# An encoder layer's branch B: output stores one unit later, splits and loads held ahead of the next unit's softmax, projection A one unit later

## The chip, the cores and the metric

The kernel runs on one core of a Trainium2 chip. The metric is the device time of one execution in microseconds (us).

## The reference

One layer of an encoder with two token mixers, applied on its own to a prompt of 1024 tokens and to a sample of 512, both 1024 wide, in float32. Cut to what matters:

```python
z = rmsnorm(x) @ W_in          # q_A k_A v_A | q_B k_B v_B (8 heads of 64) | gate_A gate_B
o_A = grouped_query_attention(rope(norm(q_A)), rope(norm(k_A)), v_A)
# branch B: per head, 128 queries against a band of rows of a 64-column grid
s = q_B . k_B[band] * 64**-0.5 + rel_pos_bias[head, dr, dc]
s = where(window(8 rows x 16 columns), s, -1e30)
o_B = softmax(s) @ v_B[band]
x = x + (sigmoid(gate_A) * (o_A @ W_pA) + sigmoid(gate_B) * (o_B @ W_pB)) @ W_out
x = x + relu(rmsnorm(x) @ W_up)**2 @ W_down
y = rmsnorm(x)
```

## The kernel before

Every float32 operand of a matmul is kept as two parts: `hi`, the value rounded by ACT (ScalarE), and `lo`, the rest, computed by DVE (VectorE). `split` (L183) makes the two, and `mm3` (L201) does a product as three matmuls. Activations lie transposed, 128 features by up to 512 tokens.

The short trunk (512 tokens, `NB == 1`) runs first, then the long one (1024 tokens, `NB == 2`), then the feed-forward part of both. A trunk does branch A in two passes, then branch B in a phase of its own (the pool `phB` at L871), then the output projection. The change acts in branch B, above all in the long trunk's, which the trace shows from about 773 to 1083 us.

Branch B is a loop over 32 units, a head `h` and a quarter `j` of the columns, with three kinds of steps, each for another unit:

- `s_unit` (L972): the scores `sbs` on PE (TensorE), bias added and the row's maximum taken on DVE (`sbss`, L1002), the exponential on ACT (`pbs`, L1024 or L1034), the division by the row's sum on POOL (GpSimd, L1037). The bias plus mask, `bms`, is added on POOL (L983).
- The turn of the probabilities, which the next product needs transposed. Heads 6 and 7 do it on PE (`ptbs`, L1076). In the long trunk heads 0 to 5 (the set `moved`, 24 units) take a detour: a 32 by 32 transpose on DVE (`turn`, L1046), a copy to DRAM issued by POOL (`tbs`, L1048), and in the next turn of the loop a fetch by four DMAs of SP (SyncE) that puts the blocks in their places (`fetch_t`, L1056, three buffers `bhs`). `t_unit` splits what was fetched, `hi` on ACT (L1066) and `lo` on DVE (L1067), three units after the scores.
- `v_unit` (L1087): the product with the values, `obs` on PE, four units after the scores; `finish_o` (L441) then adds two halves of it on ACT and DVE (`ot_Bs`, `os_Bs`) and stores the output (`obds`, L461) through `store[0]`, which is SP in the detour.

Between these steps PE is given filler work by `Fill.pull` (L48), three matmuls a pull: first branch B's gate, `gate(3328)` (matmuls `gpss`, weights `w_gs` in eight tiles, result `sgs` written by ACT and stored as `zgs` by SP), then projection A, `proj_a` (L832, matmuls `ppas`, weights `w_pas`, inputs `oXs`). A unit of head h whose index is 6 or 7 modulo 8 also does half of the query and key projections of the next two heads (`qkproj` L913, `pqbs`, `pkbs`, splits `qBs` and `kBs`). The weights and the inputs `oXs` come as raw float32 by SP into a ring of three raw tiles and are split from there; for `oXs` this is `load_o` (L818), and `oa_held` is the list of splits still to be made. `prep_v` (L894) loads a unit's values `vss`, four DMAs on SP.

Each engine does its instructions in the order that it is given. A scheduler decides this order, except where `tc.keep_in_program_order` pins it. In the long trunk's loop all matmuls are pinned (`held_pe`), so PE follows the program's text, and a late input stops it. ACT, DVE, POOL and SP are ordered by the scheduler, apart from the pins that the text shows.

Of the kernel before, what the change touches and what calls it, by code (L numbers as in the profile page):

```python
# [61 lines left out]
def encoder(ctx: ExitStack, tc: tile.TileContext, xs, outs, w):  # L62
# [119 lines left out]

    def split(hi, lo, src, pin=False):  # L183
        op = nc.scalar.activation(hi, src, AF.Copy)  # L184
        if pin:
            tc.keep_in_program_order(op)
        n = src.shape[1]
        cut = [0, n // 2, n] if n % 2 == 0 else [0, n]
        for a, b in zip(cut, cut[1:]):
            op = nc.vector.tensor_tensor(lo[:, a:b], src[:, a:b], hi[:, a:b].bitcast(F32), op=ALU.subtract)  # L190
            if pin:
                tc.keep_in_program_order(op)

    held_pe = []
# [21 lines left out]
    def load_cols(src, off, ncol, name, alloc=None, pin=False, hold=None, raw_of=None):  # L216
# [9 lines left out]
        for k0 in range(0, nk, kp):  # L226
# [3 lines left out]
            op = nc.sync.dma_start(rv, v[:, k0 : k0 + kn, off : off + ncol])  # L230
            if pin:
# [171 lines left out]
    def run(tr, nxt, first):  # L403
# [10 lines left out]
        store = [nc.scalar]  # L414

# [25 lines left out]
        def finish_o(o, n, dst, pool, nm, parts=None):  # L441
# [8 lines left out]
            else:  # L450
                nc.scalar.activation(t[:, :n], o[HD:P, :n], AF.Copy)
            if parts is not None:
                hi, lo, ps = parts
                b = pool.tile([P, n], F32, tag="os", name=f"os_{nm}", bufs=2)[ps, :n]
# [4 lines left out]
            b = pool.tile([HD, n], F32, tag="os", name=f"os_{nm}", bufs=2)  # L459
            nc.vector.tensor_tensor(b[:, :n], o[0:HD, :n], t[:, :n], op=ALU.add)  # L460
            store[0].dma_start(dst, b[:, :n])  # L461
# [356 lines left out]
        def load_o(br, hold=None, raw_of=raw_tile):  # L818
            parts = []
            for k in range(4 - br):  # L820
                raw = raw_of(f"rawo{N}_{br}_{k}")
                nc.sync.dma_start(raw[:, :T], (oad, obd)[br][k * P : (k + 1) * P, :])
                t = slot([P, 2, T], F32R, f"oX{N}_{br}_{k}", first and br + k == 0)
                cut = partial(split, t[:, 0, :], t[:, 1, :], raw[:, :T], br == 0 and NB == 2)
                if hold is None:
                    cut()
                else:
                    hold.append(cut)
# [42 lines left out]
        with phase(f"phB{N}") as ph:  # L871
# [41 lines left out]
            def qkproj(pr, wqk, dest):  # L913
# [4 lines left out]
                for tb in range(NB):  # L918
# [5 lines left out]
                    for e in range(2):  # L924
# [11 lines left out]
                        late = NB == 2 and (pr, tb) == (3, 1)  # L936
                        op = nc.scalar.activation(dst_h, src, AF.Copy, scale=0.125)
                        if late:
                            tc.keep_in_program_order(op)
                        for jj in range(4):  # L940
                            op = nc.vector.scalar_tensor_tensor(
# [7 lines left out]
                            if late:  # L949
                                tc.keep_in_program_order(op)  # L950
# [4 lines left out]
                    for e in range(2):  # L955
# [4 lines left out]
                        for os_ in both:  # L960
                            op = nc.scalar.activation(kT[e][os_, 0, cs], pk[hs], AF.Copy)
                            if NB == 2 and (pr, tb) == (3, 1):
                                tc.keep_in_program_order(op)
# [8 lines left out]
            def s_unit(u, before=None):  # L972
# [25 lines left out]
                for hf in range(halves):  # L998
# [3 lines left out]
                    nc.vector.tensor_tensor_reduce(  # L1002
                        out=sb,
                        in0=s[:, hf * 512 : hf * 512 + nkey],
                        in1=bms[hf],
                        op0=ALU.add,
                        op1=ALU.min,
                        scale=-1.0,
                        scalar=3e38,
                        accum_out=nm_,  # L1010
                    )
# [7 lines left out]
                for hf, (sb, nm_) in enumerate(sums):  # L1019
                    nm = f"{N}_{h}_{j}_{hf}"  # L1020
                    l = sml.tile([P, 1], F32, tag="l", name=f"lb{nm}")
                    if u in moved:
                        p = pm[:, :, hf]
                        nc.scalar.activation(  # L1024
                            p.rearrange("p b k i -> p k b i"),
                            sb.rearrange("p (k b i) -> p k b i", b=4, i=32),
                            AF.Exp,
                            bias=nm_,
                            scale=-1.0,
                            accum_out=l,  # L1030
                        )
                    else:
                        p = pm[:, hf * nkey : (hf + 1) * nkey]
# [888 lines left out]
```

## Time and profile before

| | us |
|---|---|
| median of three runs | 2165.71 |
| lowest, highest | 2163.8, 2169.11 |
| the profiled execution | 2162.64 |
| its span, first to last instruction | 2160.9 |
| TensorE's mean granted clock in it | 0.994 |

The time of an execution is its span and 1.7 us around it. The profile's busy times and waits are from that one execution. A row of an engine's timeline gives the start and the duration in us, the engine and line, the operation with output and inputs by the program's names, the shape, the number of instructions and, in brackets, how long the engine was idle before and what released it. A row of the waits view groups such idle times by the instruction that waited and the one that it waited for. Instructions that only issue a DMA belong to a queue, SPq for SyncE.

### The profile page before, as it was taken

Reading aid. Unit: us, or ns where it says so; the run is one execution under the profiler, and the core shown is the slowest. Engines: PE = TensorE matmul, PEld = TensorE weight load, DVE = VectorE, ACT = ScalarE, POOL = GpSimd, SP = SyncE. Lnnn points to the kernel's source line nnn. Section 1 sums busy time; section 2 is a strip of 40 time slices with the busy share of each in tenths; the row PEclk is TensorE's granted clock in tenths of the full one; section 3 lists DMA queues with packets and bytes.
Section 4 is the critical chain, followed back from the end, with each engine's and each line's share of the span. In section 5 each row is a group of like instructions: output and inputs, shape, how many; then the busy total and the mean of one; then the engine's idle time right before and its main releaser. Section 6 shows DMA issues by size and latency. Waiting matters only on the chain.

```text
span 2160.9 us, 32004 instructions
## 1 busy us (share of the span) xinstructions
PE 2104.1 (97%) x10871; PEld 1841.4 (85%) x10871; DVE 1484.3 (69%) x2793; ACT 1140.5 (53%) x2487; POOL 377.0 (17%) x470
## 2 busy tenths in 40 slices
PE   9999999999999999987999999999999999999998
PEld 8888778988898878865888899998999988888886
DVE  6665786777657746765882777777777777659662
ACT  6664654666556645544540566566555643434342
POOL 2332310332223224542200200003000000000000
PEclk9999999999999999998999999999999999999999
DMA  6437557521221146675563655578444799688561
GB/s 192 129 106 217 156 157 244 174 71 33 59 85 53 39 111 189 195 205 153 174 209 126 221 179 180 185 230 229 144 158 156 245 351 340 216 274 283 170 204 59
DMA packets 337003, 372.95 MB, mean 173 GB/s; under 512 B 33472, under 2 KB 269640, under 8 KB 336840
## 3 DMA queue, kind: packets, MB, share of 16 engines
q1 hardware_dynamic: 296695, 296.17, 44.2%
q10 hardware_dynamic: 31072, 45.11, 5.9%
q0 software_dynamic: 9072, 29.63, 4.7%
q8 instruction: 86, 1.41, 0.3%
q14 instruction: 78, 0.63, 0.1%
HBM read 274.29 MB, written 97.32 MB: 172 GB/s over the span
## 4 chain that ended last, share of the span: by engine, by line
PE 66%; DVE 1%; DMA 1%; issue 1%; ACT 1%; POOL 0%; SPq 0%; POOLq 0%; ACTq 0%; DVEq 0%
PE dn L197 20%; PE ua L197 6%; PE ud L197 6%; PE uc L197 6%; PE gpss L197 5%; PE ops L197 4%; PE ub L197 3%; PE ppbs L197 2%; PE pkbs L197 2%; PE pqbs L197 2%; PE ppas L197 2%; PE dnf L197 2%; PE pTs L791 1%; PE obs L197 1%; PE sbs L197 1%
## 5 line engine op out<-in xcount | busy, mean ns | idle before, releaser
L197 PE MATMUL dn<-wd,ah 128*128 128x512 f32 x1248 | 384.3, 389 | 0.0
L197 PEld LDWEIGHTS dn<-wd,ah 128*128 128x128 f32 x1248 | 234.4, 188 | 48.5
L197 PE MATMUL dn<-wd,al 128*128 128x512 f32 x624 | 243.0, 389 | 0.0
L1396 ACT ACTIVATE ah<-ar 128x512 fp32r<-128x512 f32 x168 | 104.1, 627 | 197.7 <-PE dn L197 183.3
L197 PE MATMUL gpss<-xs_0h,w_gs 128*128 128x512 f32 x512 | 189.3, 405 | 5.1 <-ACT w_gs L184 3.8
L1397 DVE TENSOR_TENSOR al<-ar,ah 128x512 fp32r<-128x512 f32 x168 | 114.5, 690 | 74.0 <-ACT ah L1396 63.6
L197 PE MATMUL ud<-B,A 128*128 128x384 f32 x768 | 143.7, 335 | 0.7 <-DVE c L1514 0.7
L197 PE MATMUL uc<-B,A 128*128 128x384 f32 x768 | 143.7, 334 | 0.0
L197 PE MATMUL ua<-B,A 128*128 128x384 f32 x768 | 138.8, 334 | 0.0
L197 PEld LDWEIGHTS dn<-wd,al 128*128 128x128 f32 x624 | 117.2, 188 | 24.3
L757 POOL TENSOR_SCALAR ps<-ps,rls 128x1024 f32<-128x1024 f32 (+1 forms) x96 | 96.9, 1010 | 225.5 <-DVE rls L756 200.2
L197 PEld LDWEIGHTS ud<-B,A 128*128 128x128 f32 x768 | 134.0, 188 | 1.1 <-DVE c L1514 1.1
L197 PEld LDWEIGHTS uc<-B,A 128*128 128x128 f32 x768 | 134.1, 188 | 0.2 <-ACT A L1396 0.2
L197 PEld LDWEIGHTS ua<-B,A 128*128 128x128 f32 x768 | 133.7, 188 | 0.2
L797 DVE TENSOR_TENSOR ptls<-pTs,pths 128x512 fp32r<-128x512 f32 x160 | 107.7, 687 | 37.6 <-ACT pths L796 36.8
L796 ACT ACTIVATE pths<-pTs 128x512 fp32r<-128x512 f32 x160 | 94.0, 597 | 74.0 <-PE pTs L791 71.7
L197 PE MATMUL ops<-wh_os,mgs 128*128 128x512 f32 x384 | 119.5, 391 | 0.0
L197 PEld LDWEIGHTS gpss<-xs_0h,w_gs 128*128 128x128 f32 x512 | 96.8, 190 | 24.6 <-ACT w_gs L184 4.5
L751 DVE TENSOR_REDUCE nms<-ss 128x1 f32<-128x1024 f32 (+1 forms) x96 | 99.9, 1041 | 25.5 <-PE ss L749 25.0
L180 POOL TENSOR_TENSOR rs_f<-ms_f,mhalf 128x1 f32<-128x1 f32 x6 | 4.0, 667 | 590.7 <-DVE ms_f L176 590.7
L754 ACT ACTIVATE ps<-ss,nms 128x1024 f32<-128x1024 f32 (+1 forms) x96 | 93.2, 972 | 22.7 <-DVE nms L751 20.1
L791 PEld LDWEIGHTS pTs<-ident,ps 128*128 128x128 f32 x640 | 77.9, 140 | 28.3 <-POOL ps L757 4.1
(290 smaller groups left out, 5164.6 us busy)
## 6 DMA issues: line engine op xcount, KB each, us to landing
ar<-ud SPq DMA_DIRECT2D x120, 512.0 KB, 5.1
br<-in_w_mlp_down_dram SPq DMA_DIRECT2D x72, 512.0 KB, 5.5
rawu<-in_w_mlp_up_dram SPq DMA_DIRECT2D x64, 512.0 KB, 4.1
ud<-c ACTq DMA_DIRECT2D x128, 192.0 KB, 2.9
raw_gs<-in_w_in_dram SPq DMA_DIRECT2D x32, 512.0 KB, 4.1
ud<-cs SPq DMA_DIRECT2D x64, 192.0 KB
tbs<-pbs POOLq DMA_DIRECT2D x24, 384.0 KB, 3.5
bhs<-tbs SPq DMA_DIRECT2D x96, 96.0 KB, 2.5
```

What stands on the lines that cost most here:

```text
L180: nc.gpsimd.tensor_tensor(r[:, :n], m[:, :n], mhalf[:, :n], op=ALU.pow)
L197: op = nc.tensor.matmul(out, a, b, **kw)
L751: nc.vector.tensor_reduce(nm_, s, axis=AX.X, op=ALU.max, negate=True)
L754: nc.scalar.activation(p, s, AF.Exp, bias=nm_, accum_out=l)
L757: nc.gpsimd.tensor_scalar(p, p, rl, 1.0, op0=ALU.mult, op1=ALU.mult)
L791: nc.tensor.transpose(pt[:, j * P : (j + 1) * P], PP[u, j][:, kc * P : (kc + 1) * P], ident)
L796: nc.scalar.activation(hi, pt, AF.Copy)
L797: nc.vector.tensor_tensor(lo, pt, hi.bitcast(F32), op=ALU.subtract)
L1396: nc.scalar.activation(hi, src, AF.Copy)
L1397: nc.vector.tensor_tensor(lo, src, hi.bitcast(F32), op=ALU.subtract)
```

## The change

It changes the order in which branch B's work is written, and which parts of that order the scheduler must keep. No matmul is added or removed.

1. **Output stores a unit later.** In the detour `finish_o` puts its store on a list, `later_put`; the loop issues it at its end, after `fetch_t`, and keeps the last one back until the next unit.
2. **Splits and raw loads held.** `note` records the instructions of `split` on ACT and DVE and the raw loads on SP. `behind(engine)` puts the next unit's softmax (its sum on DVE, its exponential on ACT), its fetch and its value loads on SP behind all that was recorded on that engine since.
3. **`load_o`.** In the long trunk the raw loads of pieces 2 and 3 of `oXs` are issued when pieces 0 and 1 have been split. The pins on the last query and key splits and on the `oXs` splits are gone, and so are the three `oXs` splits that stood ahead of the end of the last `qkproj`.
4. **Filler.** Nine gate matmuls (`fill.pull(3)`) stand ahead of the first unit. A unit then gets 5 pulls, one in six gets 4 (before: 5, one in three 6). Projection A is set up at unit 22 (before 23) and enters the filler at unit 25 (before 24); in the tail a unit gets 8 pulls (before 7). The `oXs` splits are made from unit 23 on, two per unit in the long trunk (before: one from unit 21). In the short trunk the same line makes them from unit 23, one per unit.

The core of the diff:

```diff
+    @contextmanager
+    def behind(engine):
+        with ExitStack() as st:
+            for ins in firm[engine]:
+                st.enter_context(tc.issue_after(ins))
+            yield
+        firm[engine].clear()
...
-            store[0].dma_start(dst, b[:, :n])
+            if store[0] is nc.scalar:
+                nc.scalar.dma_start(dst, b[:, :n])
+            else:
+                later_put.append((dst, b[:, :n]))
...
-                cut = partial(split, t[:, 0, :], t[:, 1, :], raw[:, :T], br == 0 and NB == 2)
+                def ask(k=k, t=t):
+                    raw = raw_of(f"rawo{N}_{br}_{k}")
+                    note("SP", nc.sync.dma_start(raw[:, :T], (oad, obd)[br][k * P : (k + 1) * P, :]))
+                    return partial(split, t[:, 0, :], t[:, 1, :], raw[:, :T])
...
+                elif NB == 1 or k < 2:
+                    hold.append(ask())
                 else:
-                    hold.append(cut)
+                    cuts = []
+                    early = hold[k - 2]
+                    def then(early=early, ask=ask, cuts=cuts):
+                        early()
+                        cuts.append(ask())
+                    hold[k - 2] = then
+                    hold.append(lambda cuts=cuts: cuts.pop()())
...
-                    nc.vector.tensor_tensor_reduce(
+                    with behind("DVE"):
+                        nc.vector.tensor_tensor_reduce(
...
+                    with behind("ACT"):
+                        nc.scalar.activation(to, of, AF.Exp, bias=nm_, scale=-1.0, accum_out=l)
...
+                with behind("SP"):
+                    for b in range(4):
+                        nc.sync.dma_start(
...
                 held_pe.append(1)
+                fill.pull(3)
...
-                    f = (5 if i < 2 else 2 + i % 2) if NB == 1 else 5 + (i % 3 == 0)
+                    f = (5 if i < 2 else 2 + i % 2) if NB == 1 else 5 - (i % 6 == 5)
                 else:
-                    f = 3 + i % 2 if NB == 1 else 7
-                if NB == 2 and i == n - 9:
+                    f = 3 + i % 2 if NB == 1 else 8
+                if NB == 2 and i == n - 10:
                     pa = proj_a(ph, raw_here)
                     next(pa)
-                    f = 2
...
-                        if NB == 2 and i == n - 9:
-                            for _ in range(NC8):
-                                next(qp)
-                            for _ in range(3):
-                                oa_held.pop(0)()
...
-                if NB == 2 and i == n - 8:
+                if NB == 2 and i == n - 7:
...
-                if oa_held and i > n - 12:
+                if oa_held and i >= n - 9:
                     oa_held.pop(0)()
...
                     fetch_t(units[i - 1])
+                if NB == 2 and oa_held and i >= n - 9:
+                    oa_held.pop(0)()
+                while len(later_put) > (i < n):
+                    nc.sync.dma_start(*later_put.pop(0))
```

What this does to the order shows at three places. The first is ACT in the long trunk's branch B around the last keys, before; `kBs_3_0` and `kBs_3_1` are the split keys of heads 6 and 7, `oXs_0_k` the inputs of projection A.

```order
L447 ACTIVATE ot_Bs_4_3_11495<-obs_4_3_11488 64x512
L1066 ACTIVATE bhs_5_2_11341<-bhs_5_2_11341 128x768
L184 ACTIVATE w_pas_0_11348<-raw_pas_0_0_11346 128x512
L184 ACTIVATE oXs_0_0_11351<-rawos_0_0_11349 128x1024
L184 ACTIVATE oXs_0_1_11354<-rawos_0_1_11352 128x1024
L937 ACTIVATE qBs_3_11244<-pqbs_3_1_11401 64x4x128
L184 ACTIVATE oXs_0_2_11357<-rawos_0_2_11355 128x1024
L937 ACTIVATE qBs_3_11244<-pqbs_3_1_11401 64x4x128
L961 ACTIVATE kBs_3_0_11245<-pkbs_3_1_11445 64x512 x2
L961 ACTIVATE kBs_3_1_11246<-pkbs_3_1_11445 64x512
```

The same place in the changed kernel:

```order
L1091 ACTIVATE bhs_5_1_11176<-bhs_5_1_11176 128x768
L199 ACTIVATE oXs_0_0_11185<-rawos_0_0_11186 128x1024
L971 ACTIVATE qBs_3_11226<-pqbs_3_1_11368 64x4x128 x2
L991 ACTIVATE kBs_3_0_11227<-pkbs_3_1_11403 64x512 x2
L199 ACTIVATE w_pas_0_11184<-raw_pas_0_0_11182 128x512
L991 ACTIVATE kBs_3_1_11228<-pkbs_3_1_11403 64x512
L464 ACTIVATE ot_Bs_4_3_11461<-obs_4_3_11454 64x512
L1091 ACTIVATE bhs_5_2_11322<-bhs_5_2_11322 128x768
```

Three `oXs` splits and one of `w_pas` stood ahead of the keys of `pkbs_3_1`; now one `oXs` split does, the `w_pas` split stands between the two heads' keys, and the output of unit `4_3` follows. On PE, between the last matmul of `pkbs_3_1` and `sbs_6_1`, six gate matmuls and the six of `obs_4_3` stood before; now twelve gate matmuls and those six stand there.

The second place is ACT a little further on, where projection A begins on PE: the output of unit `5_1`, the last gate result `sgs_3328_7_1`, and what follows them, before.

```order
L447 ACTIVATE ot_Bs_5_1_11549<-obs_5_1_11542 64x512
L437 ACTIVATE sgs_3328_7_1_11564<-gpss_3328_7_1_11318 128x512
L1066 ACTIVATE bhs_5_0_11501<-bhs_5_0_11501 128x768
L184 ACTIVATE w_pas_1_11569<-raw_pas_1_0_11567 128x512
L184 ACTIVATE oXs_0_3_11360<-rawos_0_3_11358 128x1024
```

And in the changed kernel, where PE does `ppas_0_0` right behind the last three matmuls of `gpss_3328_7_1`:

```order
L464 ACTIVATE ot_Bs_5_1_11553<-obs_5_1_11546 64x512
L454 ACTIVATE sgs_3328_7_1_11608<-gpss_3328_7_1_11519 128x512
L1091 ACTIVATE bhs_5_0_11466<-bhs_5_0_11466 128x768
L199 ACTIVATE oXs_0_1_11188<-rawos_0_1_11189 128x1024
L199 ACTIVATE oXs_0_2_11191<-rawos_0_2_11446 128x1024
L464 ACTIVATE ot_Bs_5_2_11600<-obs_5_2_11593 64x512
L199 ACTIVATE oXs_0_3_11192<-rawos_0_3_11474 128x1024
```

The splits of `oXs_0_1` and `oXs_0_2` have moved behind the last gate result, and `oXs_0_3` stands behind the output of unit `5_2`.

The third place is SP at the fetches of head 4, before; `obds` is the store of an output, `bhs` the fetch of turned probabilities.

```order
L461 DMA obds_4664<-os_Bs_3_0_10986 64x256
L1056 DMA bhs_4_2_10989<-tbs_4_2_10929 32x4x192 x4
L900 DMA vss_4_10802<-vds_4660 32x4x128 x4
L438 DMA zgs_1_4662<-sgs_3328_6_0_11033 128x512
L461 DMA obds_4664<-os_Bs_3_3_11058 64x256
L1056 DMA bhs_4_0_11061<-tbs_4_0_11010 32x4x192 x4
```

The same in the changed kernel:

```order
L1080 DMA bhs_4_1_10885<-tbs_4_1_10838 32x4x192 x4
L1228 DMA obds_4664<-os_Bs_3_1_10818 64x256
L935 DMA vss_4_10783<-vds_4660 32x4x128 x4
L1080 DMA bhs_4_2_10956<-tbs_4_2_10907 32x4x192 x4
L1228 DMA obds_4664<-os_Bs_3_2_10883 64x256
```

Before, the store of `os_Bs_3_0` stands ahead of the fetch of `bhs_4_2`; now that fetch stands ahead of the store of an older unit, `os_Bs_3_2`, and a store follows a fetch every time.

More of the change, by code (lines that the diff above doesn't have):

```diff
@@ L181, in rstd, with note @@
         return r
+    held_pe = []
+    firm = {"ACT": [], "DVE": [], "SP": []}
+    def note(engine, op):
+        if held_pe:
+            firm[engine].append(op.ins)
+    @contextmanager
[5 more added lines that the diff above has]
+        firm[engine].clear()
     def split(hi, lo, src, pin=False):
         op = nc.scalar.activation(hi, src, AF.Copy)
+        note("ACT", op)
         if pin:
@@ L1054, in fetch_t @@
                 turned = PT[u].rearrange("(a i) b w -> b i a w", i=32)
-                for b in range(4):
-                    nc.sync.dma_start(
-                        hl[b * 32 : b * 32 + 32, 1].rearrange("p a f k i -> p a (f k i)").bitcast(F32), turned[b]
-                    )
+                with behind("SP"):
+                    for b in range(4):
+                        nc.sync.dma_start(
+                            hl[b * 32 : b * 32 + 32, 1].rearrange("p a f k i -> p a (f k i)").bitcast(F32),
+                            turned[b],
+                        )
                 PT[u] = hl
@@ L1158, in run @@
                     if moved and h > 0:
-                        prep_v(h, j)
+                        with behind("SP"):
+                            prep_v(h, j)
                     if i % 8 == 6 and i + 2 < n:
```

62 lines of the change are left out of this document (24 added, 38 removed).

## The prediction

> **What bounds the kernel now.** I read the page's engine table first, then the waits of the tensor engine in the stretch that holds the long trunk's branch B, then that stretch cut into windows, and last the instructions of the engines around the largest waits.
>
> The page's span and its row for the tensor engine (busy time, share, instructions):
>
> ```profile
> span 2160.9 us, 32004 instructions
> PE 2104.1 (97%) x10871; PEld 1841.4 (85%) x10871; DVE 1484.3 (69%) x2793; ACT 1140.5 (53%) x2487; POOL 377.0 (17%) x470
> ```
>
> PE is the bound: only 2160.9 − 2104.1 = 56.8 us of the span are idle. A change that neither adds nor removes matmuls can win only from those, and from time at a lowered clock. How much lies where the change acts is one row of the windows view (length, then busy time of PE, PEld, DVE, ACT, POOL, the granted clock, DMA share and GB/s), and the two largest groups of PE's waits there (total, times, longest):
>
> ```profile
> 770.00:1090.00 320.00, 290.56 (x1361) 241.75 (x1360) 208.68 (x500) 150.18 (x299) 116.82 (x145) 0.97 0.60 176
> PE sbs L197 <- ACT kBs L961: 11.5, 2, 10.2
> PE obs L197 <- issue: 5.9, 3, 2.5
> ```
>
> 320.00 − 290.56 = 29.4 us idle, over half of all idle time. DVE, ACT and POOL are far from full, so each wait is a matter of order. PE's own rows place the waits above 0.5 us, and one below (start, duration, idle before and its releaser in brackets):
>
> ```profile
> 796.77 0.44 PE L197 MATMUL sbs<-kBs,qBs 128*128 128x384 f32 x1 [1.28 <-ACT kBs L961]
> 798.18 0.80 PE L197 MATMUL sbs<-kBs,qBs 128*128 128x384 f32 x3 [0.97 <-DVE kBs L965]
> 798.82 0.39 PE L197 MATMUL gpss<-xs_0h,w_gs 128*128 128x512 f32 x1
> 799.04 0.39 PE L197 MATMUL gpss<-xs_0l,w_gs 128*128 128x512 f32 x1
> ...
> 933.47 0.50 PE L197 MATMUL gpss<-xs_0h,w_gs 128*128 128x512 f32 x1 [0.92 <-ACT w_gs L184]
> 939.99 0.97 PE L197 MATMUL obs<-bhs,vss 128*128 128x256 f32 x6 [1.74 <-issue]
> 946.86 0.95 PE L197 MATMUL obs<-bhs,vss 128*128 128x256 f32 x6 [1.75 <-issue]
> 954.42 0.95 PE L197 MATMUL obs<-bhs,vss 128*128 128x256 f32 x6 [2.46 <-issue]
> 958.99 0.50 PE L197 MATMUL gpss<-xs_0h,w_gs 128*128 128x512 f32 x1 [2.90 <-ACT w_gs L184]
> 960.05 0.84 PE L197 MATMUL gpss<-xs_0h,w_gs 128*128 128x512 f32 x2 [0.33 <-DVE w_gs L190]
> 1005.99 0.69 PE L197 MATMUL sbs<-kBs,qBs 128*128 128x384 f32 x1 [10.20 <-ACT kBs L961]
> 1007.41 1.33 PE L197 MATMUL sbs<-kBs,qBs 128*128 128x384 f32 x3 [0.73 <-DVE kBs L965]
> 1018.78 1.52 PE L197 MATMUL ppas<-oXs,w_pas 128*128 128x512 f32 x2 [3.82 <-ACT oXs L184]
> 1039.26 0.96 PE L197 MATMUL obs<-bhs,vss 128*128 128x512 f32 x4 [1.50 <-DVE bhs L1084]
> ```
>
> Two gate matmuls in a row start 799.04 − 798.82 = 0.22 us apart (0.227 over a longer run); that is the price of a filler matmul as cover.
>
> **The first unit.** At 796.77 PE has just finished the keys of head pair 0 and must wait 1.28 + 0.97 = 2.25 us for their splits. The change pulls nine gate matmuls ahead of it: 9 × 0.227 = 2.05 us of work that was to be done anyway. **−2.05 us**; without that cover, 0.
>
> **The gate's weights.** 0.92 + 2.90 + 0.33 = 4.15 us are waits for splits of w_gs, which the scheduler had put behind a softmax. After, a split stands ahead of the next unit's softmax on ACT and DVE, and with fewer gate matmuls per unit the seventh weight tile is split well before its first use (the order has it twelve gate matmuls and a projection later). **−4.15 us**; I see no other end above 0.9, the smallest of the three.
>
> **The largest wait.** ACT's rows ahead of 1005.99, and the sync engine's queue that held them:
>
> ```profile
> 995.83 0.59 ACT L447 ACTIVATE ot_Bs<-obs 64x512 f32<-64x512 f32 x1 [8.19 <-PE obs L197]
> 996.33 0.83 ACT L1066 ACTIVATE bhs<-bhs 128x768 fp32r<-128x768 f32 x1
> 997.58 1.99 ACT L184 ACTIVATE oXs<-rawos 128x1024 fp32r<-128x1024 f32 x2
> 1003.05 1.06 ACT L184 ACTIVATE oXs<-rawos 128x1024 fp32r<-128x1024 f32 x1 [2.87 <-DMA rawos<-oads]
> 1004.75 1.19 ACT L961 ACTIVATE kBs<-pkbs 64x512 fp32r<-64x512 f32 x2
> 999.19 0.32 SPq L822 DMA_DIRECT2D rawos<-oads  x1
> ```
>
> The copies of the last keys (1004.75) stand behind three oXs splits, and the third waits 2.87 us for a load that SP could only issue at 999.19, when a raw buffer came free. PE, in order, waits 10.20 + 0.73 = 10.93 us. After, one oXs split is ahead of the keys and the loads for the others are asked later; between the last key matmul and sbs stand twelve gate matmuls and six obs matmuls, about 12 × 0.227 + 0.95 = 3.7 us. What they must cover is a w_pas split, the key copies and their lower halves; at the first unit the same stretch was 2.25 us after almost no cover. So **−10.9 us**; at worst the 2.25 of the first unit comes back, −8.7.
>
> **The obs waits of heads 3 and 4.** 1.74 + 1.75 + 2.46 = 5.95 us. Their probabilities travel softmax, transpose, store, fetch, split, obs. Two rows say what delays that chain: SP's queue behind the output store, and the softmax behind the copy-out of its own buffer.
>
> ```profile
> SPq L461 <- DVE os_Bs L460: 28.8, 8, 9.9
> ACT pbs L1024 <- DMA tbs<-pbs: 19.7, 8, 6.9
> 924.28 0.45 SPq L461 DMA_DIRECT2D obds<-os_Bs  x1
> 924.91 1.90 SPq L1056 DMA_DIRECT2D bhs<-tbs  x4
> ```
>
> The store at 924.28 waits for an output, and the four fetches at 924.91 queue behind it although they need it not. After, the fetch goes first and the store is one unit old. That is worth some 2 to 3 us of lead per unit, and the fetched tiles are split a unit ahead of their use. Against it: sbs's softmax is now held behind the w_gs_6 and w_bqs_3 splits, and on POOL two bias sums stand ahead of the store of head 4's first unit. The second row's wait does not go away with that. Following the new order with the durations above, I find obs_3_3 some 3.0 us late and obs_4_1 some 1.9 late: 4.9. **−1.05 us**, between −4 (only 2 us stay) and +1.5 (three units as late as the one at 954.42, 7.4 us).
>
> **The first projection.** Now 3.82 us at 1018.78. In the new order ppas_0_0 follows the last three gate matmuls directly, and ACT's queue between that last gate and the projection's inputs is: sgs, a bhs split, oXs_0_1, oXs_0_2, ot_5_2, oXs_0_3. From the last gate's start: 0.39 to its end (798.82), for sgs about the 0.59 of an output copy, 0.83 for bhs (996.33), 1.04 each for the first two oXs (1003.05), 0.59 (995.83), 1.06, and DVE's lower halves:
>
> ```profile
> L190 DVE TENSOR_TENSOR oXs<-rawos,oXs 128x512 fp32r<-128x512 f32 x8 | 5.2, 682 | 1.9 <-ACT oXs L184 1.9
> ```
>
> 5.2 / 8 = 0.65 each, behind a softmax sum and an output merge. The first half of oXs_0_3 is there some 8 us after the last gate, ppas_0_0 ends at 8.6, and undisturbed it would end at 2.97: 5.6 us instead of 3.82. **+1.8 us**, from 0 to +5 if the raw loads land late too; and +0.5 for the second w_pas (0 to 1.5).
>
> **The tail.** The 1.50 at 1039.26 is a wait for the split of a turned tile; with eight pulls instead of seven per unit more ppas matmuls stand between. **−0.7 us**, half of it either way.
>
> **The clock.** Windows of 10 us around the waits:
>
> ```profile
> 940.00:950.00 10.00, 8.25 (x43) 7.02 (x44) 6.15 (x15) 4.17 (x9) 6.57 (x8) 1.00 0.77 226
> 960.00:970.00 10.00, 9.95 (x40) 8.32 (x41) 4.49 (x12) 2.64 (x7) 2.55 (x2) 0.83 0.39 111
> 990.00:1000.00 10.00, 5.79 (x29) 4.73 (x27) 3.51 (x7) 4.15 (x6) 0.00 (x0) 0.90 0.38 134
> 1000.00:1010.00 10.00, 3.28 (x11) 2.88 (x12) 7.88 (x21) 4.12 (x7) 0.63 (x1) 0.50 0.83 236
> 1010.00:1020.00 10.00, 6.18 (x21) 4.47 (x20) 5.26 (x10) 5.03 (x10) 1.96 (x3) 0.84 0.68 197
> 1020.00:1030.00 10.00, 10.00 (x47) 8.36 (x47) 5.30 (x13) 1.83 (x5) 3.35 (x4) 0.90 0.43 126
> ```
>
> Busy time by (1 − clock): 9.95 × 0.17 + 5.79 × 0.10 + 3.28 × 0.50 + 6.18 × 0.16 + 10.00 × 0.10 = 5.9 us of work done at a lowered clock. After waits of 1.75 us (946.86) the clock stays 1.00; after 2.90 (958.99), 3.82 and 10.20 it falls. Of the waits that I expect to stay, the projection's 5.6 us is one of the second kind, and it costs about what 1018.78 costs now, 1.0 from the last row and as much again from the row before it: 2.0. **−3.9 us**, from −5.9 to −2 if an obs wait of 3.0 also lowers it.
>
> The Trainium skill (TensorE: Matmul & The Clock Gate, Part 1) has half rate after an idle window of about 3.4 µs, until about as long a busy one. By that an obs wait of 3.0 would cost nothing and each longer one 1.7 us, an estimate from its window, which makes this term −4.2. The trace half agrees: 0.50 after the 10.20, but 0.83 also after a wait of only 2.90 that followed one of 2.46.
>
> **The short trunk.** The hold on projection A's pieces is written for both trunks, so its oXs splits and two w_pas loads come later there, behind sixteen value fetches on SP:
>
> ```profile
> 276.24 12.13 SPq L900 DMA_DIRECT2D vss<-vds  x16
> ```
>
> PE has almost no wait there today. I take **+0.5 us**, from 0 to 2.3, three of the sixteen issues at 12.13 / 16 = 0.76 each.
>
> **The sum.** −2.05 − 4.15 − 10.9 − 1.05 + 1.8 + 0.5 − 0.7 − 3.9 + 0.5 = −20.0 us. The profiled execution took 2162.64 us (1.7 beside its span of 2160.9), so 2142.6; the median of the runs is 2165.71, 3.1 above it, so **2145.7**. With all bounds on the good side: −2.05 − 4.15 − 10.9 − 4 − 1.5 − 5.9 = −28.5, or 2137; on the bad side −2.05 − 3.2 − 8.7 + 1.5 + 5 + 1.5 − 0.3 − 2 + 2.3 = −6.0, or 2160. A measurement of this kernel can tell about 0.3%, 6.5 us, from no change: the bad end lies within that.
>
> **The rivals.** *New waits take most of it back.* A unit's filler falls from 5 + 1/3 pulls to 5 − 1/6, half a pull or 1.5 matmuls, 0.34 us less cover in each of 24 units, while the softmax is held longer. If in ten of the eighteen units that have no projection to hide under obs comes 1.7 us late (as at 939.99 and 946.86), 17 us are back: −3, 2163. For it: 29.4 us idle already show that obs is the fragile link. Against: of the rows above none is an obs wait of heads 0 to 2, with similar cover. Chance 0.13.
>
> *Slower.* The split that now must precede the softmax waits itself for a load, and ACT's and DVE's queues go in order:
>
> ```profile
> ACT w_pas L184 <- DMA raw_pas<-in_w_proj_a_dram: 5.5, 2, 2.9
> raw_gs<-in_w_in_dram SPq DMA_DIRECT2D x32, 512.0 KB, 4.1
> ```
>
> If a load lands 2.9 us after the softmax could start (as the worst w_pas did), that unit's probabilities are 2.9 us late, and three units on PE waits for them. About fifteen units have such a split; it decides from (20 + 6.5) / 2.9 = 9 of them on. All fifteen: −20 + 43.5 = +23.5, 2189. Against it: 4.1 us to landing is less than a unit (946.86 − 939.99 = 6.9 us with its wait, some 5 without), and the loads are asked a unit or more ahead. Chance 0.07. The Trainium skill (the same page, section on the array's architectural detail) calls the ACT and DVE queues strict first-in, first-out; by that rule nothing passes the held split, and the trace agrees in the 1004.75 row, where kBs stands behind oXs.
>
> *All of it goes.* Obs and ppas waits vanish as well: −29.4 − 5.9 + 1.3 for what is not reached = −34, 2132. It needs the three oXs splits to be done before the last gate, which the order contradicts. Chance 0.04.
>
> *The moved stores do nothing*, because the fetch waits for one of three bhs buffers anyway, not for the store. Then the 5.95 stays: −19, 2147, a case inside the forecast.
>
> **The numbers.** Forecast, −28.5 to −6: 0.76. Faster by over 0.3% is 0.76 + 0.04 = 0.80; within 0.3%, 0.13; slower 0.07. The range, 2135 to 2162, holds the forecast's own 2137 to 2160 and the edge of the first rival, and leaves out the slower case and the full gain.
>
> **What would show it.** In PE's waits after: no wait of sbs for kBs above 2.3; none of gpss for w_gs above 0.9; obs waits around heads 3 and 4 of 2 to 7.4 us in all; the largest wait left is ppas on oXs, 4 to 9 us; a lowered clock in two windows at most. Busy time in branch B stays within the clock term. I am wrong if obs waits show up in heads 0 to 2 or 5, if sbs_6_1 still waits several us, or if the short trunk loses more than 2.3 us.

## The result and the profile after

| | before | changed |
|---|---|---|
| median of four runs, us | 2166.61 | 2148.43 |
| lowest to highest | 2163.8 to 2169.11 | 2146.99 to 2151.93 |
| profiled execution, us | 2162.64 | 2149.47 |

The ratio of the runs is 0.9919, 95% interval 0.9901 to 0.9937: 18 us faster, where −20 was forecast. The two profiled executions lie 13.2 us apart, since that of before is one of its faster ones and that of the change one of its slower.

The page's first lines and the long branch B in one window, of the changed kernel:

```profile
span 2147.7 us, 32028 instructions
PE 2104.3 (98%) x10871; PEld 1840.9 (86%) x10871; DVE 1486.6 (69%) x2793; ACT 1141.4 (53%) x2487; POOL 368.6 (17%) x470
...
770.00:1090.00 320.00, 305.88 (x1434) 255.44 (x1433) 224.20 (x525) 156.74 (x310) 109.98 (x145) 0.98 0.63 187
```

PE's busy time has stayed (2104.1 before); its idle time in this stretch fell from 29.4 to 320.00 − 305.88 = 14.1 us, so −15.3. These are the waits that stay, from PE's timeline, with the last gate matmul at 1000.00, and the wait in the short trunk (the last row):

```profile
801.04 0.80 PE L212 MATMUL sbs<-kBs,qBs 128*128 128x384 f32 x3 [0.48 <-DVE kBs L993]
907.54 0.47 PE L212 MATMUL pqbs<-xs_1h,w_bqs 128*128 128x512 f32 x1 [3.50 <-DVE qBs L973]
938.08 0.95 PE L212 MATMUL obs<-bhs,vss 128*128 128x256 f32 x6 [0.48 <-issue]
946.44 1.62 PE L212 MATMUL obs<-bhs,vss 128*128 128x256 f32 x6 [3.24 <-issue]
954.67 0.96 PE L212 MATMUL obs<-bhs,vss 128*128 128x256 f32 x6 [1.78 <-issue]
1000.00 0.39 PE L212 MATMUL gpss<-xs_1h,w_gs 128*128 128x512 f32 x1
1002.81 0.49 PE L212 MATMUL ppas<-oXs,w_pas 128*128 128x512 f32 x1 [1.73 <-ACT oXs L199]
1003.78 2.85 PE L212 MATMUL ppas<-oXs,w_pas 128*128 128x512 f32 x6 [0.48 <-DVE oXs L206]
1007.80 1.22 PE L212 MATMUL ppas<-oXs,w_pas 128*128 128x512 f32 x2 [1.17 <-DVE oXs L206]
1026.90 3.01 PE L212 MATMUL ppas<-oXs,w_pas 128*128 128x512 f32 x12 [0.72 <-DVE ot_Bs L465]
1058.45 3.03 PE L212 MATMUL ppas<-oXs,w_pas 128*128 128x512 f32 x12 [0.28 <-DVE ot_Bs L465]
312.47 0.47 PE L212 MATMUL obs<-bhs,vss 128*128 128x256 f32 x2 [3.01 <-ACT ot_Bs L464]
```

No wait for w_gs is left in the long branch B, and none of sbs for the keys of heads 6 and 7: the 4.15 and 10.93 us are gone. The 3.50 of pqbs is new. The short trunk's last obs waited 1.10 us before:

```profile
309.63 0.51 PE L197 MATMUL obs<-bhs,vss 128*128 128x256 f32 x2 [1.10 <-DVE bhs L1084]
```

The windows with a lowered clock, after:

```profile
900.00:910.00 10.00, 6.50 (x30) 5.29 (x29) 8.08 (x24) 5.63 (x13) 5.55 (x8) 0.92 0.51 161
910.00:920.00 10.00, 10.00 (x42) 8.19 (x41) 4.62 (x13) 2.62 (x4) 2.10 (x4) 0.91 0.57 171
940.00:950.00 10.00, 6.76 (x28) 5.72 (x28) 6.71 (x16) 4.54 (x11) 6.90 (x10) 0.83 0.78 243
1000.00:1010.00 10.00, 6.62 (x21) 4.12 (x19) 6.57 (x15) 6.30 (x11) 3.91 (x4) 0.70 0.57 174
1010.00:1020.00 10.00, 10.00 (x48) 8.38 (x47) 7.15 (x17) 3.82 (x9) 3.65 (x5) 0.96 0.53 159
```

Busy time by (1 − clock) gives 0.5 + 0.9 + 1.1 + 2.0 + 0.4 = 5.0 us of work lost to the clock (5.9 before). Together −15.3 + 1.9 − 0.9 = −14.3 for a span that is 13.2 us shorter; 1 us of this is not found.

### The profile page after: what moved, and what is told of

The parts are those of the page before. It is cut to its first block, busy times and chain, and to the rows that moved or that the text cites. A ratio compares the mean times of both kernels' runs of the same rounds, so it can differ in the third digit from the quotient of the medians.

```text
span 2147.7 us, 32028 instructions
## 1 busy us (share of the span) xinstructions
PE 2104.3 (98%) x10871; PEld 1840.9 (86%) x10871; DVE 1486.6 (69%) x2793; ACT 1141.4 (53%) x2487; POOL 368.6 (17%) x470
## 4 chain that ended last, share of the span: by engine, by line
PE 65%; issue 1%; DVE 1%; DMA 1%; ACT 1%; POOL 0%; SPq 0%; POOLq 0%; ACTq 0%; DVEq 0%
PE dn L212 20%; PE ua L212 6%; PE ud L212 6%; PE uc L212 6%; PE gpss L212 5%; PE ops L212 4%; PE ub L212 3%; PE pqbs L212 2%; PE ppbs L212 2%; PE pkbs L212 2%; PE dnf L212 2%; PE ppas L212 1%; PE pTs L812 1%; PE obs L212 1%; PE sbs L212 1%
```

## The experiments: what each part is worth

The theory after the result was the prediction's: the later projection and the filler bring the gain (the keys, the first unit), the hold brings the 4 us of w_gs, the stores little. The rivals were that the hold, or the early fetch, carries it. Four kernels undo one part each.

**Stores at once.** Edit:

```diff
-                later_put.append((dst, b[:, :n]))
+                store[0].dma_start(dst, b[:, :n])
```

> The changed kernel, but each output store of the detour is issued at once, as before, ahead of the next fetch. Theory (the gain comes from projection A and the gate's filler, the stores matter little): 0 to 3 us above the changed kernel's 2148.4, obs waits on PE in the long branch B 1 to 3 us longer than its 5.7, the wait of DVE for an output buffer gone. Rival (the early fetch carries the gain): 8 us or more above it, with obs waits of 8 us or more in all.

Measured: 2151.29 us, ratio to the kernel before 0.9937 (0.9914 to 0.9960); it overlaps the changed kernel's interval. The obs waits are 5.7 us in all, as in the changed kernel. A wait of another kind has come:

```profile
960.59 1.48 PE L212 MATMUL sbs<-kBs,qBs 128*128 128x384 f32 x4 [4.01 <-DVE nmbs L1031]
```

PE wants the scores of unit `5_0` and has no bank, since the softmax sum of `5_1` hasn't been done. Neither theory had this; the rival of an early fetch has fallen. The wait of pqbs, 3.50 us in the changed kernel, is 0.69 here: the later store avoids the one wait and brings the other, so against stores at once it gains little, 2.9 us between the medians.

**No hold.** Edit:

```diff
-            firm[engine].append(op.ins)
+            pass
```

> The changed kernel, but nothing is held ahead of the next unit's softmax, fetch or value loads. Theory: the waits of gpss for w_gs come back with 3 to 4 us, the wait of 3.5 us of pqbs may go, together 0 to 5 us above the changed kernel. Rival (the hold carries the gain): 10 us or more above it. Second rival (the hold costs more than it gives): 2 us or more below it.

Measured: 2161.51 us, 0.9979 (0.9969 to 0.9989): 13 us of the 18 are lost, and the theory with them; it is the first rival's case. No w_gs wait came back. Three of the waits of PE that came instead:

```profile
938.13 1.62 PE L212 MATMUL obs<-bhs,vss 128*128 128x256 f32 x6 [5.70 <-issue]
968.56 0.50 PE L212 MATMUL pkbs<-xs_0h,w_bks 128*128 128x512 f32 x1 [1.63 <-ACT w_bks L199]
1023.31 0.73 PE L212 MATMUL ppas<-oXs,w_pas 128*128 128x512 f32 x2 [3.31 <-ACT w_pas L199]
```

Splits of weights run late, and at 938 a fetched tile stands behind a gate split on DVE. The clock loss is 10.3 us by the same sum over windows, where the changed kernel had 5.0.

**The old projection.** Edit: `load_o`, its pins, the three early splits, the set-up at unit 23 and the start at unit 24 as before.

```diff
-                if NB == 2 and i == n - 10:
+                if NB == 2 and i == n - 9:
                     pa = proj_a(ph, raw_here)
                     next(pa)
+                    f = 2
...
-                if NB == 2 and i == n - 7:
+                if NB == 2 and i == n - 8:
...
-                if oa_held and i >= n - 9:
+                if oa_held and i > n - 12:
```

> The changed kernel, but projection A is set up and begun one unit earlier, its inputs are loaded and split as before, with the pins of before; stores, holds and the amounts of filler as changed. Theory: the wait of sbs for kBs before the first unit of head 6 comes back with 8 to 10 us, the clock is lowered behind it again, 11 to 15 us above the changed kernel, about 2161. Rival (the holds alone order the keys ahead of the oXs splits): less than 4 us above it.

Measured: 2153.75 us, 0.9944 (0.9925 to 0.9963), some 5 above the changed kernel, between the two expectations. The keys' wait came back, smaller:

```profile
994.95 0.69 PE L212 MATMUL sbs<-kBs,qBs 128*128 128x384 f32 x1 [7.01 <-ACT kBs L996]
996.78 1.33 PE L212 MATMUL sbs<-kBs,qBs 128*128 128x384 f32 x3 [1.14 <-DMA bhs<-tbs]
```

8.15 us instead of 10.93, and some 2.6 us of small waits beside it; but of the 3.38 us of ppas waits for oXs 0.23 are left, and the short trunk's last obs waits 1.10 again instead of 3.01. So the later projection is worth 8.15 + 2.6 and costs 3.1 + 1.9, so 5.7 in all, near the 5 of the medians.

**The old filler.** Edit:

```diff
-                fill.pull(3)
...
-... NB == 1 else 5 - (i % 6 == 5)
+... NB == 1 else 5 + (i % 3 == 0)
...
-... NB == 1 else 8
+... NB == 1 else 7
```

> The changed kernel, but with the old amounts of filler: no gate matmuls ahead of the first unit, 5 or 6 pulls per unit, 7 in the tail. Theory: the 2.25 us at the first unit are back, and the gate runs out one or two units earlier, so that little cover is left around the last keys: 2 to 8 us above the changed kernel. Rival (more cover per unit is worth more than the first unit's 2 us): obs waits shorter by 3 us, the same time or less.

Measured: 2155.98 us, 0.9956 (0.9942 to 0.9969), 7.6 above the changed kernel, as the theory had it in time. Of its two reasons one is there: the 2.25 us at the first unit are back. No wait for the last keys came; instead sbs waits twice for a softmax sum (3.24 and 2.48 us), and the obs of 1006.75 waits 2.94.

Undone one at a time, the four parts cost 2.9, 13.1, 5.3 and 7.6 us. That is 28.9 in all, where the whole change gave 18.2.

**One part alone.** The hold seemed the largest part, so it was tried on the kernel before; then the filler, then both. The edits are the reverse of those above.

> The kernel before with only the hold added: splits and raw loads stand ahead of the next unit's softmax, fetch and value loads; stores, projection A and filler as before. New theory (the hold is the largest part, since without it 13 us of the 18 were lost): 8 to 13 us under the kernel before, with the waits of gpss for w_gs gone and obs waits under 6 us. Rival (the hold only pays with the new filler and the later projection): under 4 us gained, the wait of sbs for kBs still 10 us and obs waits as before or longer.

Measured: 2170.43 us, 1.0023 (1.0013 to 1.0033): slower by 5. The theory has fallen. The rival fits as far as it goes (nothing gained, the keys' wait there), but it named no loss; this is the prediction's slower rival, though by another cause. PE, ACT and DVE of this kernel around the first of two such waits, in that order:

```profile
926.91 0.87 PE L212 MATMUL sbs<-kBs,qBs 128*128 128x384 f32 x4
931.04 0.89 PE L212 MATMUL obs<-bhs,vss 128*128 128x256 f32 x6
935.94 1.65 PE L212 MATMUL sbs<-kBs,qBs 128*128 128x384 f32 x4 [4.01 <-DVE nmbs L1038]
```
```profile
931.97 0.59 ACT L464 ACTIVATE ot_Bs<-obs 64x512 f32<-64x512 f32 x1
932.46 1.04 ACT L199 ACTIVATE w_gs<-raw_gs 128x1024 fp32r<-128x1024 f32 x1
```
```profile
933.65 1.28 DVE L206 TENSOR_TENSOR w_gs<-raw_gs,w_gs 128x512 fp32r<-128x512 f32 x2
934.85 0.54 DVE L1038 CUSTOM_DVE_ANT_0 sbss<-sbs,bms 128x384 f32<-128x384 f32 x1
```

The gate's split stands on ACT behind the copy of an output, `ot_Bs`, and that copy waits for the obs of 931.04. The held softmax sum stands behind the split, so it runs at 934.85, some seven us after its scores at 926.91, and PE, right behind that obs, finds both banks of scores full. The order turns a free choice into a chain: obs, copy, split, sum, sbs. The keys' wait of 10.29 stays as before. The waits for w_gs are gone with the hold alone.

> The kernel before with only the new amounts of filler: nine gate matmuls ahead of the first unit, 5 pulls per unit and one in six 4, 8 in the tail. Theory (the waits for w_gs come from the gate running ahead of its weights, so fewer pulls remove them without any hold): w_gs waits under 1 us, the first unit's wait 0.5, the wait of sbs for kBs still 9 to 11; 4 to 9 us under the kernel before. Rival (the w_gs waits need the hold): 2 us under it.

Measured: 2161.46 us, 0.9985 (0.9976 to 0.9994). The w_gs waits are gone without any hold, as the theory had it, and the first unit's wait is 0.48; but an obs wait of 6.51 us stands at 938, where before had 1.74 at 940, and only 3.4 us are gained, less than the theory's 4 to 9.

> The kernel before with the hold and the new filler; stores and projection A as before. Theory (the hold stalls sbs behind a held softmax sum only where a gate split falls in the wrong unit, which the new filler moves): no wait of sbs for the sum above 1 us, 6 to 10 us under the kernel before. Rival (the later store is what lets the hold pay): waits of sbs for the sum of 4 us are back, less than 4 us under the kernel before.

Measured: 2155.35 us, 0.9955 (0.9940 to 0.9971), as expected in time. Of the mechanism half is true: of the two waits of sbs for the sum one is gone, the other, 4.01 us, is there, and the obs waits of heads 3 and 4 are 2.23, 2.60 and 1.73 us instead of 6.51, 0.43 and 1.84.

So hold and filler are worth +5 and −3 alone, and −10 together. Parts of an order don't add up. The keys' wait, too, depends on both: 10.29 us with the hold, 9.88 with the filler, 7.64 with the two.

**Which engines the hold needs.** Edit: `note` records nothing for SP.

> The changed kernel with the hold on ACT and DVE alone; SP's raw loads are ordered freely. Theory (what the hold gives comes from the loads being asked in time, so that no split is late at the head of ACT's queue): most of the 13 us that the kernel without any hold lost are lost here too, 2156 to 2161. Rival (it comes from the splits standing ahead of the softmax on ACT and DVE): 2147 to 2151, as the changed kernel.

Measured: 2150.13 us, 0.9934 (0.9919 to 0.9949), the rival's case: what counts is the splits ahead of the softmax on ACT and DVE, not when the loads are asked. Which of the two engines needs it, no run tells.

## The experiments: the later store, and two mends

**A store in the same unit.** Edit: behind the fetch, but not kept back.

```diff
-                while len(later_put) > (i < n):
+                while later_put:
```

> The changed kernel, but a unit's output store is issued right behind the fetch of the same turn of the loop, not one unit later. Theory (a store that is a unit old keeps one of the two output buffers, and DVE waits 2.4 us for it at 933 us): that wait goes, the obs waits of heads 3 and 4 fall from 5.5 to 2 to 4 us, 1 to 4 us under the changed kernel. Rival (SP now waits for the output and delays the value loads and the next fetch): obs waits of 6 us or more, the same time or up to 4 us above it.

Measured: 2156.05 us, 0.9957 (0.9942 to 0.9972), 7.6 above the changed kernel; both expectations missed. DVE no longer waits for an output buffer, but the obs waits of heads 3 and 4 are 5.4 us, against 5.5 without the edit, and sbs waits 3.91 us for the sum of `5_1`. So the fetch's place ahead of the store does not pay by itself; what the edit took away is the unit by which a store is late.

**Two mends.** The new wait of pqbs is for a bank of matmul results that is freed late: on ACT the second half of the queries stood behind a key copy. In the changed kernel:

```profile
904.07 0.59 ACT L991 ACTIVATE kBs<-pkbs 64x512 fp32r<-64x512 f32 x1 [2.96 <-PE sbs L212]
...
905.42 0.59 ACT L971 ACTIVATE qBs<-pqbs 64x512 fp32r<-64x512 f32 x1
```

With stores at once that copy ran later still (906.88) and pqbs didn't wait for it (it began at 905.45), so it must have had another bank there: the wait needs the late copy and the bank, not the copy alone.

The wait of the short trunk was put down to the later oXs splits. Edit:

```diff
-                if oa_held and i >= n - 9:
+                if oa_held and i >= (n - 11 if NB == 1 else n - 9):
...
-                        nc.scalar.activation(dst_h, src, AF.Copy, scale=0.125)
+                        last_q = nc.scalar.activation(dst_h, src, AF.Copy, scale=0.125)
...
+                            with tc.issue_after(last_q.ins) if held_pe else ExitStack():
                                 nc.scalar.activation(kT[e][os_, 0, cs], pk[hs], AF.Copy)
```

> The changed kernel with two mends: in the short trunk the oXs splits are made two units earlier again, and in the long trunk ACT writes the keys of a head pair only after the second half of its queries. Theory: the wait of 3.0 us of the short trunk's last obs falls to about 1.1, as before; the wait of 3.5 us of pqbs, and the lowered clock behind it (1.4 us of work), go; together 5 to 7 us under the changed kernel, about 2142. Rival for the second (DVE's turn for the queries is late by itself, since it also serves the softmax sums): pqbs still waits 2 us or more and only 2 us are gained.

Measured: 2142.52 us, 0.9900 (0.9885 to 0.9915), the fastest kernel here. Both rows are as expected, the second not wholly, and the lowered clock at 900 to 920 is gone:

```profile
309.60 0.51 PE L212 MATMUL obs<-bhs,vss 128*128 128x256 f32 x2 [1.10 <-DVE bhs L1110]
902.06 0.47 PE L212 MATMUL pqbs<-xs_1h,w_bqs 128*128 128x512 f32 x1 [1.03 <-DVE qBs L973]
```

**A third output buffer**, on top of the mends: with stores a unit late, DVE waited 2.44 us at 933 us for one of two output buffers (the row is the changed kernel's; with the mends it is 2.37 us):

```profile
933.07 0.42 DVE L478 TENSOR_TENSOR os_Bs<-ot_Bs 64x256 f32<-64x256 f32 x1 [2.44 <-DMA obds<-os_Bs]
```

The edit also takes four buffers each from two small tiles of the norms, to make room:

```diff
-            n_os = 2
+            n_os = 3 if NB == 2 else 2
...
+        m = sml.tile([P, 8], F32, tag="ms", name=f"ms_{name}", bufs=4)
...
+        r = sml.tile([P, 8], F32, tag="rs", name=f"rs_{name}", bufs=4)
```

> The changed kernel with the two mends of the short trunk and the queries, and a third buffer for a unit's output (room for it by four instead of eight buffers of two small tiles of the norms). Theory (a store a unit old keeps one of two output buffers, DVE waits 2.4 us for it and the softmax sum of head 4 behind it): that wait goes, the obs waits of heads 3 and 4, 5.4 us, fall by 1.5 to 3 us, 2 to 5 us under the kernel with the two mends, about 2139. Rival (the softmax waits for the copy of its own buffer to DRAM, whatever the output buffers do): obs waits within 1 us of 5.4, the same time.

Measured: 2151.41 us, 0.9940 (0.9927 to 0.9952): 9 us slower than with the mends alone. DVE's wait for the buffer is gone, as the theory had it, but the obs waits have grown from 5.4 to 6.6 us, and pqbs waits 2.88 instead of 1.03, so theory and rival have both fallen. Its ACT and PE:

```profile
958.93 0.59 ACT L464 ACTIVATE ot_Bs<-obs 64x512 f32<-64x512 f32 x1 [3.53 <-PE obs L212]
959.43 1.04 ACT L199 ACTIVATE w_gs<-raw_gs 128x1024 fp32r<-128x1024 f32 x1
```
```profile
958.01 0.89 PE L212 MATMUL obs<-bhs,vss 128*128 128x256 f32 x6
962.81 1.65 PE L212 MATMUL sbs<-kBs,qBs 128*128 128x384 f32 x4 [3.91 <-DVE nmbs L1032]
```

It is the chain of the hold alone. In the changed kernel the split of w_gs_7 stands ahead of the copy of output `4_2`:

```profile
956.83 1.06 ACT L199 ACTIVATE w_gs<-raw_gs 128x1024 fp32r<-128x1024 f32 x1 [0.52 <-DMA raw_gs<-in_w_in_dram]
...
962.67 0.58 ACT L464 ACTIVATE ot_Bs<-obs 64x512 f32<-64x512 f32 x1
```

The late store keeps the output buffers busy, and with only two of them the scheduler puts the next copy further back, behind the split: this reading is argued from the orders. The kernel with the mends has the changed kernel's order too, and differs from this one in the buffers alone. With stores at once, with stores in the same unit and with a third buffer the copy stands ahead of it, and sbs waits 4.01, 3.91 and 3.91 us.

**The copies held by name.** If that is all, the copy can be held behind the splits directly, with stores at once. Edit, on the mends and stores at once:

```diff
+                with ExitStack() as st:
+                    for ins in firm["ACT"]:
+                        st.enter_context(tc.issue_after(ins))
                     nc.scalar.activation(tv, o[HD:P], AF.Copy)
```

> The kernel with both mends, but with each output store issued at once, and with the copy of a unit's output out of PSUM on ACT also held behind the splits made so far. Theory (the later store helps only because it keeps a buffer busy and so pushes the copy of the output of unit 4_2 behind the split of the last gate weights; put there directly, the copy does the same): no wait of sbs for the softmax sum, where the stores at once had one of 4.0 us; 2138 to 2143, the level of the two mends or below. Rival (the later store pays by itself, through earlier fetches): the wait of sbs for the sum may go, but obs waits grow by 3 us or more over the 5.4 of the two mends, 2145 or more.

Measured: 2153.98 us, 0.9941 (0.9927 to 0.9956). Both expectations failed: the copy stands behind the split, obs waits are 5.8 us, hardly more, and yet sbs waits:

```profile
962.10 1.65 PE L212 MATMUL sbs<-kBs,qBs 128*128 128x384 f32 x4 [2.89 <-DVE nmbs L1035]
957.78 1.06 ACT L199 ACTIVATE w_gs<-raw_gs 128x1024 fp32r<-128x1024 f32 x1 [4.77 <-DMA raw_gs<-in_w_in_dram]
958.86 0.59 ACT L467 ACTIVATE ot_Bs<-obs 64x512 f32<-64x512 f32 x1
```

ACT stood 4.77 us at the split, since its raw tile landed at 957.78; PE was 1.3 us earlier here (its obs of `4_1` at 953.37, 954.67 in the changed kernel). That is the cause that the prediction's slower rival named, in one unit. But the edit does more than it was meant to: it holds every copy, and the copies of `3_3` and `4_1`, which the changed kernel does ahead of this split, at 953.60 and 955.71, stand behind it too (the copy at 958.86 is that of `3_3`). So this kernel hasn't the changed kernel's order, and the theory of the one copy `4_2` is neither shown nor refuted. PE's waits of 0.25 us and more are 18.9 us here against 11.1 with the mends alone, and the clock loss 5.1 against 4.3: 8.6 of the 12.0 us between the two spans. What the late store gives, and by which way, stays open.

## Why the prediction was right, point by point

The time came out as forecast: −20.0 worked out, −18.2 between the medians, 2148.43 in the range of 2135 to 2162. The terms can be checked only in the profiled executions, which lie closer together: that of before is 4.0 us under its runs' median, that of the change 1.0 over its own. In us (the tail's 1.74 is 1.50 and a wait of 0.24 at 1036.78):

| term | forecast | measured |
|---|---|---|
| first unit | −2.05 | 0.48 − 2.25 = −1.8 |
| gate's weights | −4.15 | −4.15 |
| largest wait | −10.9 | −10.9 |
| obs, heads 3 and 4 | −1.05 | 5.50 − 5.95 = −0.45 |
| projection | +2.3 | 3.38 − 3.82 = −0.4 |
| tail | −0.7 | 1.00 − 1.74 = −0.7 |
| clock | −3.9 | −0.9 |
| short trunk | +0.5 | +1.9 |
| not foreseen: pqbs | 0 | +3.5 |
| sum | −20.0 | −13.9 |

That −20.0 and −18.2 lie so near is in part luck. For the pair of profiled executions, from which the terms were taken, the forecast is 6 us too large. The rest of the 18.2 lies in runs without a profile, and of these the record has, beside their times, only the mean clock: 53 other executions of the kernel before had 0.990 to 0.994, with a median of 0.992, where the profiled one had 0.994; the change's four had 0.995 to 0.997. A thousandth of the clock is at most 2.1 us of PE's 2104 busy us (an estimate), so the 0.002 can be up to 4 us. Between the medians the clock's term was then probably larger than the −0.9 of this pair; no profile shows by how much.

- The obs waits were found where the order had put them: 3.0 and 1.9 late were foretold for the two, 3.24 and 1.78 measured. That a reading of the order by durations goes so far is the best of it.
- The projection came out where it was foretold, under two heads: ppas_0_0 ends 1007.80 + 1.22 − 1000.00 = 9.0 us after the start of the last gate matmul, 8.6 forecast. Of the 6.0 us above the undisturbed 2.97, 3.38 are waits and most of the rest is work at half clock, which the table has in the clock's row. The second w_pas cost nothing.
- Mis-sized: the clock's term, the step by which one of the waits that stay would lower it, at 2.0 us. Three did: pqbs (1.4 us of work lost), obs (1.1) and ppas (2.4), 5.0 in all. So the sign "a lowered clock in two windows at most" failed: there are five.
- Missed: pqbs. I followed the queues around the old waits, not around a place that had none. It is a new wait of the first rival's kind, and the only large one in the long branch B. With 3.50 us it is the largest that is left, where ppas on oXs had been named for that, with 4 to 9; the longest of ppas is 1.73.
- Within its bounds of 0 to 2.3, but not shown in its reason: the short trunk. The profile has the wait end with an output copy on ACT, and ACT's copies there stand behind an oXs split that waited 1.53 us for its load at 308.74, twenty us after the sixteen value fetches were issued (until 288.64). Splits made two units earlier brought it back to 1.10.
- Two slips in the sum of the bounds: the good end takes −1.5 for the tail, whose own bound is −1.05, and the bad end leaves out that the first unit could give 0. Put right, the ends are 2137.7 and 2161.8, still within the range.
- Wrong in its reasons, not in its sum: the change part by part. The w_gs waits were put down to the hold and the fewer pulls together; either alone removes them. The store was to give 2 to 3 us of lead per unit; the obs waits were no longer without it. And the hold, for which no gain was booked beyond w_gs, is worth 13 us in the changed kernel and costs 5 by itself. The step that failed is taking each edit's worth from the waits of before: the edits share one order, and most of what each does shows only beside the others.
- The slower rival, at 0.07, had the right place (a held sum, and PE behind it) and needed nine units; alone, the hold has it in two, 4.01 us each. Its cause there is an output copy ahead of the split rather than a late load; only the last experiment shows the load.

The Trainium skill (TensorE: Matmul & The Clock Gate, Part 1) has the clock halved after an idle window of about 3.4 µs. The trace is stricter on what lowers it. Windows of the changed kernel at the projection:

```profile
1000.00:1002.00 2.00, 1.07 (x5) 0.56 (x3) 0.16 (x1) 1.52 (x3) 0.00 (x0) 1.00 0.59 206
1002.00:1004.00 2.00, 0.71 (x2) 0.41 (x3) 2.00 (x4) 1.98 (x3) 0.00 (x0) 1.00 0.32 81
1004.00:1006.00 2.00, 2.00 (x5) 1.25 (x5) 2.00 (x6) 1.26 (x2) 0.00 (x0) 0.51 0.55 162
1006.00:1008.00 2.00, 0.83 (x3) 0.20 (x2) 2.00 (x8) 1.30 (x4) 1.91 (x2) 0.50 0.62 192
1008.00:1010.00 2.00, 2.00 (x9) 1.70 (x9) 0.41 (x1) 0.24 (x1) 2.00 (x3) 0.50 0.75 231
```

The clock is 0.51 from 1004 on, after waits of 1.73 and 0.48 us with half a microsecond of work between them: 4 us that were 1.78 busy went before it, without one long gap.

How long it stays lowered comes in steps. In the windows of 10 us, (1 − clock) × 10 us is 0.8 + 0.9 = 1.7 us after pqbs, 1.7 after the obs wait and 3.0 + 0.4 = 3.4 at the projection; at a clock of a half that is 3.4, 3.4 and 6.8 us of time. The same sum over neighbouring windows is a multiple of 1.7, within 0.1, in the traces of all the kernels here (1.7 and 8.6 before). So each time the clock fell it cost up to 1.7 us of work, and less where PE was idle.

## What to carry to other kernels

Price an edit of order by where it puts each instruction among its neighbours, not by the wait that it is meant for: hold and filler gave +5, −3 and together −10 us. A rule that holds one instruction behind another also holds it behind all that stands in front of that one; look there for anything that waits for the engine you want to free. And room can change an order for the worse: with a third buffer the kernel was 9 us slower, so after adding room, read the order again.

## What the runs showed of the hardware

DVE's subtraction of a 128x512 half of w_gs takes 1.28 us for two (933.65 above). Without the hold, one pair took 3.58 us, while POOL worked from 933.06 to 936.61, and the fetched tile for the obs of 938.13 stood behind it:

```profile
933.58 3.58 DVE L206 TENSOR_TENSOR w_gs<-raw_gs,w_gs 128x512 fp32r<-128x512 f32 x2 [0.15 <-ACT w_gs L199]
937.08 0.94 DVE L1092 TENSOR_TENSOR bhs<-bhs 128x768 fp32r<-128x768 f32 x1
```
```profile
933.06 1.80 POOL L1060 TENSOR_SCALAR pbs<-pbs,rlbs 128x384 f32<-128x384 f32 x2
934.84 1.77 POOL L1011 TENSOR_TENSOR bms<-rects,msks 128x384 f32<-128x384 f32 x2
```

The filler alone has the same pair at 933.64 with 3.79 us, and POOL at work from 933.49 to 936.87; the obs wait of 6.51 us follows it. In the timelines of all the runs here, from 770 to 1090 us, 80 such pairs of weight tiles met no POOL work, and none took over 1.30 us. The seven pairs of over 3 us all had 2 us or more of POOL work beside them; 28 others that had 1.0 to 1.7 took 1.29 to 1.71. That POOL is what slowed DVE is still argued from the times; no run took POOL's work away.
